# Storing a normalized operand by token class, and keys and values feature by feature

## The chip, the cores and the metric

The kernel runs on one core of a Trainium2 chip. The metric is the device time of one execution in microseconds; "us" below is always that. Three runs of the kernel before took 1931.80, 1932.94 and 1935.67 us, so the median is 1932.94 us. One further execution was recorded by the profiler, and every row below is from it.

The engines are named as in the profile: PE is TensorE (matmuls), PEld its loads of the stationary operand, DVE is VectorE, ACT is ScalarE, POOL is GpSimd, SP is SyncE, which issues most DMAs.

## The reference, cut to what matters

512 tokens of width 1024 pass through two stacks of layers. Only the first layer of the first stack is touched by the change. It normalizes the tokens and projects them:

```python
hn = rms_norm(h, norm_g[0])
q, k, v, gate_a, u, gate_b = split_cols(hn @ w_in, (512, 128, 128, 512, 512, 512))
q = rms_norm(q.reshape(b, L, 8, 64), q_g)
k = rms_norm(k.reshape(b, L, 2, 64), k_g)
att = swa_sink_attention(q, k, v, sinks, rel_bias) * silu(gate_a)
ssm = s5_mixer(u, log_dt, a_re, a_im, b_re, b_im, c_re, c_im, d, glu_w, glu_b) * silu(gate_b)
h = h + concatenate([att, ssm], axis=-1) @ w_out
```

`s5_mixer` is a linear recurrence over the tokens: 32 groups of 16 channels, 64 complex states each, `x[t] = A x[t-1] + B u[t]`, `y = Re(C x) + d u`, then a gelu and a gated product. The matrices A and B are worked out from small parameter tables (`log_dt`, `a_re`, `a_im`, ...) with exponentials, sines and powers. The rest of the network (a sparse attention layer, then two layers with forgetting and dilated attention and wide feed-forward parts) takes most of the time and isn't touched.

## The kernel before, in words

**Products.** Numbers are f32, split into a high and a low part in the engine's own 32-bit type. A product is three matmuls (`mm3`, lines 210, 211 and 212): high by high, high by low, low by high. There are two forms. In `tm` (token-major) 128 tokens of x are the stationary operand, and 256 weight columns move past it. In `fm` (feature-major) 128 weight columns are stationary, and the tokens move. With eight blocks of 128 input features, a `tm` of 128 tokens by 256 features is 24 matmuls. `slab` fetches 256 weight columns through two raw buffers on SP's queue and splits them: ACT makes the high part (line 204), DVE the low part (line 206).

**The operand.** `norm_block` scales a block of 128 tokens (`tb`, four of them), and `to_x` transposes it on PE into PSUM (line 266). ACT copies the high part to `xh` (line 268), and DVE subtracts to make `xl` (line 269). Column t of `x1` is token t.

**Order of the first layer.** The program text goes: for each block of tokens, normalize, project keys and values (`tm`, 24 matmuls), normalize the key heads (`head_norm`: ACT squares, DVE sums, POOL takes the power for 1/sqrt in 0.7 us, DVE scales, lines 394 to 399), transpose the keys to `kT` (line 436, tile `ft`); then the state space parameters: PE transposes the tables `prm` (line 460), DVE copies them to `pt` (line 462), and a long chain of small DVE and ACT operations makes the powers `pw`, the matrices `bb`, the tables `uu` and `et`, and at last `zb` (lines 466 to 614); meanwhile PE makes the state space input `u2` (192 matmuls). For this input the recurrence is cut in four token classes, token = 4 j + i, so the stationary operand of class i is every fourth column of `x1`:

```python
tm(ps[:, :256], w, lambda k: tuple(
    a[k // 4][:, k % 4].rearrange("p (j i) -> p i j", i=4)[:, i] for a in (x1.h, x1.l)))
```

Then follows the core of the state space layer in four quarters (`core_a`, `core_b`): `core_a(0)` transposes `zb` on PE (line 641) and makes the tile `c` (`c7`, line 650); the last half ends with the transposes of `gy` (line 735). After that come the queries (192 matmuls with a head norm for each block), the gates `gbt` and `gat` (192 matmuls with 512 moving columns, `fm`, then `silu2`, line 779), the gated product (its first matmul has `yh` as an operand), and the attention.

**What sets the order.** This text isn't executed as it stands. A scheduler fixes, when the program is built, one order for each engine, and fills gaps of one part with work of another: part of the query matmuls stand between those of the core. At run time each engine goes through its list strictly, and an instruction that waits holds all that stand behind it. Tiles come from pools with few buffers, and an accumulator (`acc`) in PSUM can be written again only when ACT or DVE has copied it out; for `u2` these copies are lines 358 (DVE) and 360 (ACT).

Of the kernel before, what the change touches and what calls it, by code (L numbers as in the profile page):

```python
# [8 lines left out]
F32 = mybir.dt.float32  # L9
# [88 lines left out]
def _build(tc, nc, ctx, t, out, dbg, upto):  # L98
# [158 lines left out]
        x.l = [xp.tile([128, 4, 512], F32R, tag="x", name="xl") for _ in range(2)]  # L257
        return x

    def to_x(xn, hdst, ldst, nk=8, tags=("tps", "tps")):  # L260

        for half in range(nk // 4):
            ps = pst(tags[half])
            pv = ps.rearrange("p (k t) -> p k t", k=4)
            for k in range(4):
                PE.transpose(pv[:, k], xn[:, (half * 4 + k) * 128:(half * 4 + k + 1) * 128], ident)
            h_ = hdst(half)
            A.activation(h_, pv, AF.Copy)  # L268
            V.tensor_tensor(ldst(half), pv, h_.bitcast(F32), op=OP.subtract)  # L269

    def norm_block(hb, gb, x, tb, tags=("tps", "tps"), pl=None, put_off=None):
        xn = (pl or nrm).tile([128, 1024], F32, tag="xn", name="xn")
        norm_scale(hb, gb, xn)
        sl = slice(tb * 128, (tb + 1) * 128)

        def rest():
            to_x(xn, lambda hf: x.h[hf][:, :, sl], lambda hf: x.l[hf][:, :, sl], tags=tags)
        if put_off:
            put_off(rest)
        else:  # L280
            rest()
# [78 lines left out]
            A.activation(dst, src, AF.Copy)  # L360


    st1 = ExitStack()
    l1 = phase(st1, "l1")
    n0x = ExitStack()
# [57 lines left out]
    V.tensor_copy(qgs, qg)  # L423
    V.tensor_scalar(qgs[:, 0:1], qg[:, 0:1], -0.125, None, op0=OP.mult)
    V.tensor_scalar(qgs[:, 2:3], qg[:, 2:3], -float(np.float32(128 ** -0.5)), None, op0=OP.mult)
    for tb in range(NB):
        norm_block(xin[tb], gb, x1, tb, pl=n0)
        sl = slice(tb * 128, (tb + 1) * 128)
        ps = acc()
        tm(ps[:, :256], w, xk(x1, tb * 128, tb * 128 + 128))  # L430
        kn2 = pj.tile([128, 2, 2, 64], F32, tag="kn2", name="kn2", bufs=2)
        head_norm(ps[:, :128], 2, 64, [kn2[:, :, q] for q in range(2)])
        evac(vt[:, tb], ps[:, 128:256])
        tp = pst("ft")
        for i in range(2):
            PE.transpose(tp[:, i * 128:(i + 1) * 128], kn2[:, i].rearrange("p a d -> p (a d)"), ident)
        A.activation(kT[:, :, sl], tp[:, :256].rearrange("p (a t) -> p a t", a=2), AF.Copy, scale=qgs[:, 1:2])
    bias_tables(n0, (sps(), sps()))
    n0x.close()
    dump("x1h", x1.h[0])  # L440
# [124 lines left out]
    w = 2  # L565
# [13 lines left out]
    for cs_ in range(2):  # L579
        w = slab(w_in1, 0, 8, [(1280 + cs_ * 256, 256)])  # L580
        for i in range(4):
            ps = acc()
            tm(ps[:, :256], w, lambda k: tuple(
                a[k // 4][:, k % 4].rearrange("p (j i) -> p i j", i=4)[:, i] for a in (x1.h, x1.l)))
            evac(u2[:, cs_ * 16:(cs_ + 1) * 16, i, :], ps[:, :256].rearrange("p (g x) -> p g x", x=16))
    dump("u2", u2)
    shm = nrm.tile([128, 1024], F32, tag="gb", name="shm").rearrange("p (t c) -> p t c", t=8)
# [170 lines left out]

    for cs_ in range(2):
        w = slab(w_in1, 0, 8, [(cs_ * 256, 256)])  # L760
        for tb in range(NB):
            sl = slice(tb * 128, (tb + 1) * 128)
            ps = acc()
            tm(ps[:, :256], w, xk(x1, tb * 128, tb * 128 + 128))
            qn = pj.tile([128, 4, 64], F32, tag="qn", name="qn", bufs=2)
            head_norm(ps[:, :256], 4, 64, [qn])
            steps.tick()
            steps.later(1, lambda a=(qn, cs_, sl): q_turn(*a))
# [6 lines left out]
    def silu2(pl, dst, ps):  # L775

        th_ = pl.tile([128, 512], F32, tag="th", name="th_", bufs=1)
        A.activation(th_, ps, AF.Tanh, scale=0.5)
        V.scalar_tensor_tensor(dst, th_, 1.0, ps, op0=OP.add, op1=OP.mult)

    gbt = ytp.tile([128, 4, 512], F32, name="gbt")
    for cs_ in range(2):
# [827 lines left out]
```

## Time and profile before

| What | Value |
| --- | --- |
| Median of three runs | 1932.94 us |
| Profiled execution, its own time | 1937.1 us |
| Span of its records | 1935.2 us |
| Mean granted TensorE clock | 0.971 |
| PE busy | 1833.9 us, 95% of the span, 11098 instructions |
| DVE busy | 1039.4 us, 54% |
| ACT busy | 728.6 us, 38% |
| POOL busy | 132.9 us, 7% |
| DMA | 161.74 MB, mean 84 GB/s |
| Chain that ended last | PE 81%, DVE 7%, issue 4%, DMA 3%, ACT 3%, POOL 1% |

Read it so: PE is busy nearly all the time, so the kernel as a whole hangs on PE, and the chain that ended last runs through PE for four fifths of the span. But these are averages over the whole network. The change touches about the first 220 us, and there the limits are different in each stretch; they have to be read from the rows of those stretches. The profiled execution is 4.2 us longer than the median (1937.1 against 1932.94 us).

### The profile page before, as it was taken

The numbers are of one execution on the slowest core, as the hardware profiler recorded it, in microseconds if no ns is written. First come the engines' busy times: TensorE is split into PE (matmuls) and PEld (weight loads), VectorE is DVE, ScalarE is ACT, GpSimd is POOL, SyncE is SP. The second block draws the span as 40 slices with busy tenths as digits, with TensorE's granted clock in tenths as the row PEclk, the third lists the DMA queues.
The fourth block names the chain that finished last, engine by engine and source line by source line (L and its number), as shares of the span: only waits on it lengthen the run. The fifth ranks groups of instructions, "written<-read, shape, count | busy, mean of one in ns | idle before, by whom it ended". The sixth has DMA issues, their size and how long they took to land.

```text
span 1935.2 us, 27920 instructions
## 1 busy us (share of the span) xinstructions
PE 1833.9 (95%) x11098; PEld 1540.4 (80%) x11100; DVE 1039.4 (54%) x2199; ACT 728.6 (38%) x1454; POOL 132.9 (7%) x151
## 2 busy tenths in 40 slices
PE   6999969999999999999999999999989899999998
PEld 5987759859789887678888888889957788888886
DVE  5874474268664534664655553366275555555522
ACT  4133353333443334543443341233264444333421
POOL 1332001203120000000000000000000000000000
PEclk9999989969999999989999999999999999999999
DMA  6112321301521432102333322333220043322321
GB/s 207 44 34 88 131 66 51 98 22 56 166 72 41 149 109 77 33 1 66 110 100 88 101 74 98 110 130 98 78 87 1 3 120 98 99 87 82 115 87 66
DMA packets 187898, 161.74 MB, mean 84 GB/s; under 512 B 14568, under 2 KB 170320, under 8 KB 187768
## 3 DMA queue, kind: packets, MB, share of 16 engines
q1 hardware_dynamic: 181168, 144.30, 24.1%
q0 software_dynamic: 2784, 9.00, 1.5%
q10 hardware_dynamic: 3816, 6.66, 1.0%
q8 instruction: 88, 1.44, 0.3%
q14 instruction: 42, 0.34, 0.1%
HBM read 157.88 MB, written 4.74 MB: 84 GB/s over the span
## 4 chain that ended last, share of the span: by engine, by line
PE 81%; DVE 7%; issue 4%; DMA 3%; ACT 3%; POOL 1%; ACTq 0%; POOLq 0%; DVEq 0%; SPq 0%
PE acc L212 19%; PE acc L210 19%; PE acc L211 19%; PE misc L338 6%; PE o L338 3%; PE tps L338 2%; PE spp L338 2%; DVE wl L206 1%; PE sps L1064 1%; PE misc L210 1%; PE misc L211 1%; PE misc L212 1%; PE o L1140 1%; ACT wh L204 1%; DVE xn L247 1%
## 5 line engine op out<-in xcount | busy, mean ns | idle before, releaser
L206 DVE TENSOR_TENSOR wl<-raw,wh 128x1024 fp32r<-128x1024 f32 (+3 forms) x250 | 299.1, 1207 | 408.2 <-ACT wh L204 407.3
L204 ACT ACTIVATE wh<-raw 128x1024 fp32r<-128x1024 f32 (+2 forms) x262 | 270.3, 1044 | 475.6 <-PE acc L211 208.9
L212 PE MATMUL acc<-xh,wl 128*128 128x512 f32 (+2 forms) x1032 | 391.0, 380 | 4.3 <-DVE wl L206 4.3
L210 PE MATMUL acc<-xh,wh 128*128 128x512 f32 (+2 forms) x1032 | 391.6, 381 | 0.7 <-ACT xh L268 0.5
L211 PE MATMUL acc<-xl,wh 128*128 128x512 f32 (+2 forms) x1032 | 391.0, 380 | 0.0
L212 PEld LDWEIGHTS acc<-xh,wl 128*128 128x128 f32 (+1 forms) x1032 | 193.9, 188 | 45.0 <-DVE wl L206 5.9
L210 PE MATMUL acc<-wh,xh 128*128 128x256 f32 (+1 forms) x736 | 224.5, 305 | 3.0 <-ACT xh L268 2.8
L210 PEld LDWEIGHTS acc<-xh,wh 128*128 128x128 f32 (+1 forms) x1032 | 193.1, 188 | 40.7 <-ACT xh L268 1.0
L211 PEld LDWEIGHTS acc<-xl,wh 128*128 128x128 f32 (+1 forms) x1032 | 193.8, 188 | 38.0
L211 PE MATMUL acc<-wl,xh 128*128 128x256 f32 (+1 forms) x736 | 220.6, 300 | 1.1 <-DVE wl L206 1.1
L212 PE MATMUL acc<-wh,xl 128*128 128x256 f32 (+1 forms) x736 | 220.2, 300 | 0.8 <-DVE xl L269 0.8
L210 PEld LDWEIGHTS acc<-wh,xh 128*128 128x128 f32 x736 | 152.5, 207 | 10.1 <-ACT xh L268 5.8
L212 PEld LDWEIGHTS acc<-wh,xl 128*128 128x128 f32 x736 | 152.7, 208 | 6.0 <-issue 4.3
L211 PEld LDWEIGHTS acc<-wl,xh 128*128 128x128 f32 x736 | 152.7, 207 | 4.9 <-issue 3.3
L212 PE MATMUL acc<-wh,gl 128*128 128x512 f32 x352 | 139.2, 395 | 0.0
L210 PE MATMUL acc<-wh,gh 128*128 128x512 f32 x352 | 138.6, 394 | 0.0
L211 PE MATMUL acc<-wl,gh 128*128 128x512 f32 x352 | 138.6, 394 | 0.0
L245 POOL TENSOR_TENSOR rs<-ss,mhalf 128x1 f32<-128x1 f32 x32 | 17.6, 552 | 1479.2 <-DVE ss L243 1470.2
L338 PE MATMUL misc<-wh,ah 128*128 128x256 f32 x280 | 83.0, 296 | 0.0
L338 PE MATMUL misc<-wl,ah 128*128 128x256 f32 x280 | 80.1, 286 | 0.0
L338 PE MATMUL misc<-wh,al 128*128 128x256 f32 x280 | 79.9, 285 | 0.0
L211 PEld LDWEIGHTS acc<-wl,gh 128*128 128x128 f32 x352 | 66.2, 188 | 15.6
(1494 smaller groups left out, 3057.1 us busy)
## 6 DMA issues: line engine op xcount, KB each, us to landing
raw<-in_w_up_dram SPq DMA_DIRECT2D x176, 256.0 KB, 3.1
raw<-in_w_down_dram SPq DMA_DIRECT2D x44, 512.0 KB, 3.6
raw<-in_od_w_in_dram SPq DMA_DIRECT2D x24, 512.0 KB, 3.5
raw<-in_w_in_dil_dram SPq DMA_DIRECT2D x20, 512.0 KB, 3.6
raw<-in_ev_w_in_dram SPq DMA_DIRECT2D x18, 512.0 KB, 4.0
raw<-in_w_out_dram SPq DMA_DIRECT2D x16, 512.0 KB, 3.9
raw<-in_w_in_fox_dram SPq DMA_DIRECT2D x14, 512.0 KB, 4.8
raw<-in_ev_w_out_dram SPq DMA_DIRECT2D x8, 512.0 KB, 4.2
```

The costliest lines, as they stand in the source:

```text
L204: A.activation(hi[:, k0:k1], raw, AF.Copy)
L206: eng.tensor_tensor(lo[:, k0:k1], raw, hi[:, k0:k1].bitcast(F32), op=OP.subtract)
L210: pe.matmul(ps, lh, rh, start=first, stop=False)
L211: pe.matmul(ps, lh, rl, start=False, stop=False)
L212: pe.matmul(ps, ll, rh, start=False, stop=last)
L245: G.tensor_tensor(r, ss[:, 3:4], mhalf[:, :1], op=OP.pow)
L247: V.scalar_tensor_tensor(xn[:, hv[i]], hb[:, hv[i]], r, gb[:, hv[i]], op0=OP.mult, op1=OP.mult)
L338: self.last = op(*a, **k).ins
L1064: PE.matmul(ps[:, :n], qiT[rw, hd // 2, qs], kiT[rw, :n], start=True, stop=True)
L1140: PE.matmul(pov[:, hd % 4], vt[:, kb, kv * 128:(kv + 1) * 128], pt_[:, kb * 128:(kb + 1) * 128], start=kb == 0, stop=kb == qb)
```

## The change

1. The first layer's operand `x1` is stored by token class: column i * 128 + tb * 32 + j holds token 4 (32 tb + j) + i. So the copies to `xh` and `xl` read PSUM with every fourth element and write 32 neighbouring columns for each class (`norm_block1`, and the new argument `view` of `to_x`).
2. The state space input takes `xk(x1, i * 128, i * 128 + 128)`, neighbouring columns, as its stationary operand. Its 192 matmuls remain 192.
3. Keys and values are now made for two blocks of tokens at a time, in feature-major form: 24 matmuls for the keys and 24 for the values with 256 moving tokens, 96 in all as before. The result is copied from PSUM into token order (`kvf`, 4 copies), and 8 transposes on PE (line 462 of the changed kernel) bring it back to tokens by features; head norm and the rest follow as before.
4. The queries run over classes instead of blocks, and their transposed result goes to every fourth column of `qT`.
5. `silu2` writes its result back into token order (8 operations on 128x512 elements, with a stride of four elements).

Behind the change, lines have other numbers: 460 is now 492 (tables), 490 is 522 (first power), 614 is 645 (`zb`), 641 is 672, 650 is 681, 735 is 766, 755 is 786.

```diff
-    def to_x(xn, hdst, ldst, nk=8, tags=("tps", "tps")):
+    def to_x(xn, hdst, ldst, nk=8, tags=("tps", "tps"), view=lambda a: a):
...
+            pv = view(pv)
             h_ = hdst(half)
             A.activation(h_, pv, AF.Copy)
             V.tensor_tensor(ldst(half), pv, h_.bitcast(F32), op=OP.subtract)
...
+    def by_i(ap):
+
+        return ap.rearrange("p (j i) -> p i j", i=4)
+
+    def norm_block1(hb, gb, x, tb, pl):
+        xn = pl.tile([128, 1024], F32, tag="xn", name="xn")
+        norm_scale(hb, gb, xn)
+
+        def dst(a):
+            return a.rearrange("p k (i t j) -> p t k i j", i=4, t=NB)[:, tb]
+        to_x(xn, lambda hf: dst(x.h[hf]), lambda hf: dst(x.l[hf]),
+             view=lambda pv: pv.rearrange("p k (j i) -> p k i j", i=4))
+
+    def xhalf(x, half):
+
+        return lambda k: tuple(a[k // 4][:, k % 4].rearrange("p (i j) -> p i j", i=4)[:, :, half * 64:half * 64 + 64]
+                               for a in (x.h, x.l))
...
-    for tb in range(NB):
-        norm_block(xin[tb], gb, x1, tb, pl=n0)
-        sl = slice(tb * 128, (tb + 1) * 128)
-        ps = acc()
-        tm(ps[:, :256], w, xk(x1, tb * 128, tb * 128 + 128))
...
+    for half in range(2):
+        for tb in (2 * half, 2 * half + 1):
+            norm_block1(xin[tb], gb, x1, tb, n0)
+        kvf = []
+        for part in range(2):
+            ps = acc()
+            fm(ps[:, :256].rearrange("p (i j) -> p i j", i=4), w, part * 128, 128, xhalf(x1, half))
+            f_ = n0.tile([128, 256], F32, tag=f"kvf{part}", name="kvf", bufs=1)
+            evac(by_i(f_), ps[:, :256].rearrange("p (i j) -> p i j", i=4))
+            kvf.append(f_)
+        for q in range(2):
+            tb = 2 * half + q
+            sl = slice(tb * 128, (tb + 1) * 128)
+            ps = sps()
+            for part in range(2):
+                PE.transpose(ps[:, part * 128:(part + 1) * 128], kvf[part][:, q * 128:(q + 1) * 128], ident)
...
-            tm(ps[:, :256], w, lambda k: tuple(
-                a[k // 4][:, k % 4].rearrange("p (j i) -> p i j", i=4)[:, i] for a in (x1.h, x1.l)))
+            tm(ps[:, :256], w, xk(x1, i * 128, i * 128 + 128))
...
-        for tb in range(NB):
-            sl = slice(tb * 128, (tb + 1) * 128)
+        for i in range(4):
+            sl = slice(i, 512, 4)
             ps = acc()
-            tm(ps[:, :256], w, xk(x1, tb * 128, tb * 128 + 128))
+            tm(ps[:, :256], w, xk(x1, i * 128, i * 128 + 128))
...
-        V.scalar_tensor_tensor(dst, th_, 1.0, ps, op0=OP.add, op1=OP.mult)
+        th_, ps = (a.rearrange("p (i j) -> p i j", i=4) for a in (th_, ps))
+        V.scalar_tensor_tensor(by_i(dst), th_, 1.0, ps, op0=OP.add, op1=OP.mult)
```

The scheduler's order changes with it in three places that matter below. In the rows, a name's number is that of its buffer, the operands stand as moving, then stationary, and "x3" is three instructions in a row.

First, PE's list where the tables `prm` are transposed, which opens the chain of small operations. Before, it stands among the key and value matmuls of the second block of tokens (`acc_254`):

```order
L172 MATMUL sps_426<-oh_427,rel_429 8x128
L210 MATMUL acc_254<-wh_133,xh_105 128x256
L211 MATMUL acc_254<-wl_134,xh_105 128x256
L460 MATMUL sps_447<-ident_90,prm_125 128x16 x3
L436 MATMUL ft_226<-ident_90,kn2_214 128x128 x2
L212 MATMUL acc_254<-wh_133,xl_107 128x256
```

In the changed kernel the same transposes (line 492) stand behind the last keys (`ft_441`), inside the second accumulator of the state space input (`acc_670`):

```order
L468 MATMUL ft_422<-ident_90,kn2_410 128x128 x2
L172 MATMUL sps_445<-oh_447,rel_449 8x512
L468 MATMUL ft_441<-ident_90,kn2_429 128x128 x2
L172 MATMUL sps_446<-oh_447,rel_449 8x128
L210 MATMUL acc_670<-wh_634,xh_105 128x256
L211 MATMUL acc_670<-wl_635,xh_105 128x256
L492 MATMUL sps_467<-ident_90,prm_125 128x16 x3
L212 MATMUL acc_670<-wh_634,xl_107 128x256
```

So the tables have moved from the second of four blocks to the place behind all four.

Second, PE's list at the end of the state space input. Before, the transposes of `zb` follow its last matmul (`acc_816`) at once, and the first query (`acc_1470`) begins between them:

```order
L211 MATMUL acc_816<-wl_729,xh_106 128x256
L212 MATMUL acc_816<-wh_728,xl_108 128x256
L641 MATMUL tps_871<-ident_90,zb_846 128x128 x4
L647 MATMUL sps_883<-cbd_524,zb_846 128x32
L210 MATMUL acc_1470<-wh_1460,xh_105 128x256
```

In the changed kernel 71 query matmuls (`acc_1490`, `acc_1525` and 23 of `acc_1564`) stand ahead of the same transposes, now line 672:

```order
L211 MATMUL acc_1564<-wl_1481,xh_106 128x256
L672 MATMUL tps_891<-ident_90,zb_866 128x128 x4
L678 MATMUL sps_903<-cbd_544,zb_866 128x32
L212 MATMUL acc_1564<-wh_1480,xl_108 128x256
L786 MATMUL ft_1599<-ident_90,qn_1550 128x128 x2
```

What moved is query work, from behind the core to a place ahead of it. At the core's end (line 735, now 766) 54 query matmuls and all 192 gate matmuls stood behind it before; now no query matmul does, and 174 gate matmuls.

Third, DVE's list in the changed kernel, in the middle of the chain of small operations (`uu`, `et`). The copy of `acc_810`, a finished accumulator of the state space input, stands there; its buffer is the one that the first query, `acc_1490`, is to use:

```order
L537 TENSOR_TENSOR et_555<-ctmp_587,ctmp_588 128x16x4
L590 SCALAR_TENSOR_TENSOR uu_494<-uu_494 128x16
L359 COPY u2_633<-acc_810 128x16x16
L591 TENSOR_TENSOR uu_494<-sc_473 128x16
L534 TENSOR_TENSOR ctmp_597<-et_555,uu_494 128x256
```

The copy comes behind the sixth squaring of `uu` (line 590), far down the chain. Two head norms of queries stand in the same list further on, ahead of the first `zb`; before, none did.

SP's list is the same but for one place: the load of `dm` (the table with d, 256 KB) stands behind two more weight loads (`raw_1482` and `raw_1486`, 512 KB each) than before.

## Rows read from the trace of the kernel before

**Rows 1.** Chain of waits (start, duration, engine, tile, line), 87 to 97 us.

```profile
87.31 0.23 PE acc L212
...
92.44 0.44 PE tps L641 x4
```

**Rows 2.** Busy time of each engine (instructions), granted clock, DMA share, GB/s, three stretches.

```profile
40.00:42.00 2.00, 2.00 (x11) 2.00 (x11) 0.00 (x0) 0.22 (x1) 0.00 (x0) 0.50 1.06 372
...
60.00:70.00 10.00, 10.00 (x44) 10.00 (x45) 9.83 (x16) 0.38 (x1) 9.61 (x9) 1.00 0.00 0
...
100.00:160.00 60.00, 56.66 (x669) 48.22 (x670) 45.95 (x95) 20.71 (x35) 20.23 (x21) 0.97 0.15 45
```

**Rows 3.** Groups by line, 60 to 92 us: the state space input's matmuls and weight loads.

```profile
L210 PE MATMUL acc<-wh,xh 128*128 128x256 f32 x46 | 18.2, 396 | 0.0
...
L210 PEld LDWEIGHTS acc<-wh,xh 128*128 128x128 f32 x46 | 15.2, 330 | 0.0
```

**Rows 4.** Timeline of TensorE and its loads: keys and values, then the state space input.

```profile
40.15 0.41 PE L210 MATMUL acc<-wh,xh 128*128 128x256 f32 x1
...
41.86 0.41 PE L212 MATMUL acc<-wh,xl 128*128 128x256 f32 x1
...
42.27 0.28 PE L211 MATMUL acc<-wl,xh 128*128 128x256 f32 x1
...
43.10 0.28 PE L212 MATMUL acc<-wh,xl 128*128 128x256 f32 x1
...
42.51 0.19 PEld L211 LDWEIGHTS acc<-wl,xh 128*128 128x128 f32 x1
...
56.33 0.40 PE L212 MATMUL acc<-wh,xl 128*128 128x256 f32 x1
...
59.84 0.40 PE L212 MATMUL acc<-wh,xl 128*128 128x256 f32 x1
```

**Rows 5.** Timeline of VectorE, 43 to 96 us, with idle time and releaser.

```profile
43.88 0.69 DVE L572 TENSOR_TENSOR dm<-dm,mkd 128x512 f32<-128x512 f32 x1 [5.72 <-DMA dm<-in_ev_ssm_d_dram]
...
44.49 0.18 DVE L490 TENSOR_TENSOR pw<-sc 128x16 f32<-128x16 f32 x1
...
83.97 0.69 DVE L614 TENSOR_TENSOR zb<-ctmp 128x512 f32<-128x512 f32 x1
...
86.02 0.69 DVE L614 TENSOR_TENSOR zb<-ctmp 128x512 f32<-128x512 f32 x1
...
92.48 0.42 DVE L358 COPY u<-acc 128x256 f32<-128x256 f32 x1 [5.77 <-PE acc L212]
...
95.41 0.29 DVE L650 TENSOR_TENSOR c<-sps,dm 128x128 f32<-128x128 f32 x1 [1.31 <-PE sps L647]
```

**Rows 6.** Timeline, 23 to 39 us: TensorE, then ScalarE.

```profile
23.41 0.35 PE L460 MATMUL sps<-ident,prm 16*128 16x16 f32 x3
...
37.62 0.69 PE L436 MATMUL ft<-ident,kn 128*128 128x128 f32 x2 [4.24 <-DVE kn L399]
...
33.95 0.22 ACT L466 ACTIVATE sc<-pt 128x16 f32<-128x16 f32 x1
...
38.72 0.20 ACT L482 ACTIVATE sc<-sc 128x16 f32<-128x16 f32 x1
```

**Rows 7.** Single lines' instructions, strided and contiguous writes: shortest, median and longest ns.

```profile
L740 DVE TENSOR_TENSOR yl<-tps,yh x4: 1075/1103/1169, 135.2 to 164.7; 128x512 fp32r<-128x512 f32 x4
...
L269 DVE TENSOR_TENSOR xl<-tps,xh x24: 677/680/692, 14.2 to 1573.2; 128x512 fp32r<-128x512 f32 x24
```

**Rows 8.** Timeline of TensorE, 161 to 218 us.

```profile
161.78 1.09 PE L735 MATMUL tps<-ident,gy 128*128 128x128 f32 x8 [0.91 <-DVE gy L728]
...
174.56 0.41 PE L755 MATMUL ft<-ident,qn 128*128 128x128 f32 x2 [1.32 <-DVE qn L399]
...
217.04 0.40 PE L212 MATMUL acc<-xh,wl 128*128 128x512 f32 x1
217.27 0.40 PE L210 MATMUL acc<-yh,wh 128*128 128x512 f32 x1
```

More of the change, by code (lines that the diff above doesn't have):

```diff
@@ L425, in _build @@
     V.tensor_scalar(qgs[:, 2:3], qg[:, 2:3], -float(np.float32(128 ** -0.5)), None, op0=OP.mult)
-    for tb in range(NB):
-        norm_block(xin[tb], gb, x1, tb, pl=n0)
-        sl = slice(tb * 128, (tb + 1) * 128)
-        ps = acc()
-        tm(ps[:, :256], w, xk(x1, tb * 128, tb * 128 + 128))
[L431 to L437, printed above, removed]
+    for half in range(2):
[14 more added lines that the diff above has]
+                PE.transpose(ps[:, part * 128:(part + 1) * 128], kvf[part][:, q * 128:(q + 1) * 128], ident)
+            kn2 = pj.tile([128, 2, 2, 64], F32, tag="kn2", name="kn2", bufs=2)
+            head_norm(ps[:, :128], 2, 64, [kn2[:, :, r] for r in range(2)])
+            evac(vt[:, tb], ps[:, 128:256])
+            tp = pst("ft")
+            for i in range(2):
+                PE.transpose(tp[:, i * 128:(i + 1) * 128], kn2[:, i].rearrange("p a d -> p (a d)"), ident)
+            A.activation(kT[:, :, sl], tp[:, :256].rearrange("p (a t) -> p a t", a=2), AF.Copy, scale=qgs[:, 1:2])
     bias_tables(n0, (sps(), sps()))
```

## The prediction

> **What bounds the kernel now.** I read the chain of waits first: ahead of 92 us it runs through the matmuls of the state space input, link after link of `acc`, and on into the transposes of `zb`, the core's first step [rows 1]. So in this stretch PE is the path. The view by windows agrees: from 60 to 70 us PE and its weight loads are busy for 10.00 of 10.00 us at a granted clock of 1.00 [rows 2], which is TensorE's upper level, 2.4 GHz. DVE is nearly as full there (9.83 us), with the chain of small operations that makes `zb`; that is the second candidate for the bound. Its timeline says how close it is: it starts with line 490 at 44.49 us (queued behind `dm`, whose DMA it waited 5.72 us for), ends the first `zb` at 83.97 + 0.69 = 84.66, the second at 86.02 + 0.69 = 86.7, and then DVE is idle for 5.77 us until PE gives it the last accumulator at 92.48 [rows 5]. PE reaches the core 7.6 us after `zb` is there. A faster PE is worth that much in this place, and anything beyond it only if DVE's chain is earlier too.
>
> Next the matmuls themselves. For the state space input, one of 128x256 takes 396 ns and its weight load 330 ns [rows 3], and they follow each other every 0.234 us: 15 steps from 56.33 to 59.84. The same shape for keys and values, whose stationary columns are neighbours, follows every 0.119 us, 7 steps from 42.27 to 43.10, with a load of 0.19 us [rows 4]. The Trainium skill's page "TensorE: Matmul & The Clock Gate", section "LDWEIGHTS (loading the stationary operand)", lets a load's time hang on the number of its columns alone; by it both loads would take the same, and the change would save nothing here. The trace, with 330 and 190 ns for 128 columns each, doesn't agree.
>
> **What the change removes.** 192 x (0.234 - 0.119) = 22.1 us of PE time. That is for a clock of 1.00 only: at a granted clock of 0.50 (1.2 GHz, 40 to 42 us [rows 2]) neighbouring columns follow every 0.21 us (8 steps from 40.15 to 41.86 [rows 4]), so almost nothing is saved there.
>
> **What it adds on PE.** Eight 128x128 transposes: a pair takes 0.41 us [rows 8] to 0.69 [rows 6], so 1.6 to 2.8 us. The 96 key and value matmuls stay, with other operands.
>
> **What it adds on ACT and DVE.** The 8 + 8 copies to `xh` and `xl` read and write with gaps. Contiguous, `xl` takes 0.68 us; the nearest strided row is `yl`, 1.10 us for the same size [rows 7]. So each costs between nothing and 0.42 us more, and I price ACT's like DVE's (an estimate). I take half: only the writes of `yl` skip, with a wider gap. The page "Advanced Engine Details and Errata" of the Trainium skill, section "Memory Cachelines", says that PSUM is read in lines of two f32 values, so every fourth value is a new line; by it the upper price holds, some 7 us more in all, of which the path would carry about 4. No row before shows such a read. Four copies `kvf` (0.42 us each by the accumulator's copy [rows 5], up to 0.7 strided) lie on the key path. The strided `silu2`, 8 times at most 0.42 us more, lies on DVE under gate matmuls of 24 x 0.23 us per tile, and costs nothing; without that cover it would cost 3.4 us.
>
> **What it moves.** The tables `prm` are transposed at 23.41 us and used by ACT at 33.95 [rows 6]. In the new order they stand on PE behind all keys. My hand schedule, from rows of like instructions (estimates): keys and values now need two normalized blocks, so they begin at about 18.6 us; 48 matmuls at 0.21 falling to 0.12 end at 26.4; copies, transposes and head norm (POOL's power 0.7 among them) end near 30; DVE makes the last `xl` of the second half at 33.6; its 48 matmuls, first at 0.21, end at 41.1; then the copy, two weight splits of 1.2 us on DVE, head norm and transposes, with the state space input waiting behind the keys' transposes on PE. So the tables come at 48.3, the copy `pt` at 48.7, and the small chain from line 466 to line 482 (4.97 us from 33.95 to 38.92 [rows 6], with other work between, 4.1 without) leads to line 522 at 52.8. `dm` lands about then as well: it stood ready at 43.88, and is moved past two loads on SP (some 4 us each). Before, line 490 was at 44.49; **the chain starts 8.3 us later**. From there to the first `zb` it is 84.66 - 44.49 = 40.2 us as before; one key head norm moves out (-1.5, with its wait), one copy (0.4) and two query head norms (2.0) move in. First `zb`: 52.8 + 40.2 + 0.9 = 93.9; before it was 84.66.
>
> PE meanwhile: 192 x 0.119 = 22.9 us from 41.1, with some 3.7 for waits at the keys and the lower clock: done at 67.7. Then the first query needs the buffer of `acc_810`, whose copy stands behind the sixth squaring on DVE, 27.1 us into the chain: 52.8 + 27.1 = 79.9. So PE is idle for 12 us; the queries run from there to about 93, at 0.21 or 0.12 us each. **PE's bound goes over to DVE's chain.** The core's transposes come at 93.9 instead of 92.28. The tile `c` (95.41 before) needs the second `zb` too, at 96.0, and two short groups of matmuls behind it: 97.7.
>
> **The core and the tail.** From `c` to the last transposes of `gy` it took 161.78 + 1.09 - 95.41 = 67.5 us, with PE busy for 56.66 of 60 us [rows 2], so I let it hang on PE's work: 16 or 17 query matmuls fewer (-2.0), 18 gate matmuls more (18 x 0.23 = 4.1): 97.7 + 67.5 + 2.2 = 167.4, instead of 162.87. Behind that point stood 54 queries, with stalls for head norms (1.32 at 174.56) and the gates, whose run at 0.23 (217.04, 217.27) ends at 217.27 [rows 8]: 54.4 us. Now there are 174 gate matmuls: 174 x 0.23 = 40.0. The gated product begins at 207.4.
>
> **The sum.** 217.27 - 207.4 = **9.9 us** gained; of 22.1 saved on PE, 12 go to the later chain. Later layers keep their order but for pieces; I give them nothing, and 2 us of uncertainty. The profiled execution's 1937.1 becomes 1927.2; it stands 4.2 above the median, which goes from 1932.94 to 1923.0. About 0.2%, 3.9 us, can be told from no change: faster is below 1929.1, slower above 1936.8.
>
> The bounds: with the tables transposed as soon as PE is through at the upper clock, line 522 comes at 48, and 14.7 us are gained; with all strided copies and the lower clock on the path it comes at 58, and 4.7 are gained. The own range of this case is 1918 to 1928.
>
> **The rivals.**
> - *PE stays the path.* If the scheduler's late places cost little at run time and the chain starts within 4 us of before, the core starts at 85 to 89 us and nearly all of the 22 us arrive: 1911 to 1918. For it: DVE was idle for 5.77 us. Against it: the order itself, tables behind all keys. Chance 0.12.
> - *The loss eats the gain.* Line 522 at 58 to 66: gain 4.7 to -3.7, 1928 to 1936.6. For it: the keys' path has POOL powers, two groups of waits (4.24 us at 37.62 [rows 6] before), and PE idles into its lower clock. Chance 0.17.
> - *Slower*, by one mechanism: the copies that read PSUM with gaps. All of ACT's and DVE's copies stand in series ahead of both halves of keys. At 1.1 us they add 4; to pass 66.6 us, from which it is slower than 1936.8, they must add 13.8, that is 1.7 us for each of 8 pairs, about twice the strided row's whole excess for both engines. Only if such reads are that much slower: about 1943 at 2.5 us. Chance 0.10.
> - *Stride isn't what makes the load slow.* Then the input stays at 192 x 0.234 = 44.9 us and ends at 89.7; 71 queries, ahead of the core now, lead to 98.0; the core ends 4 us later than forecast, and the gain is 5.8, only by the shorter tail: 1927. It is what the section on LDWEIGHTS named above would make of it; rows 4 speak against it. Chance 0.05.
> - My forecast: 0.56.
>
> Counted together: faster 0.72 (forecast, PE's path, the stride rival, a little of the second), within 0.2% 0.17, slower 0.11. The range 1912 to 1933 leaves out a part of the first rival and the slower half of the second with the third, 0.18 in all.
>
> **What would show it.** Right: loads of about 190 ns and a pitch of 0.12 in the input; a stretch of some 10 us before the core in which PE waits for a copy on DVE; line 522 at 48 to 58; `zb` (line 645) as the releaser of line 672; gates without queries behind line 766. Wrong: line 522 before 47 (more gain) or behind 60 (less); `xl` copies (line 270) of over 1.2 us; a core that takes longer than 70 us from line 681 to line 766, as queries and gates now sit elsewhere in it; or a gate run that stalls because its weights are split too late.

## The result, and the profile after

Four runs of the changed kernel took 1909.78 to 1915.12 us, with a median of 1912.51; four of the kernel before, on the same chip, 1931.80 to 1935.67, with a median of 1932.71. The ratio is 0.9895 [0.988, 0.9911]: 20.2 us faster. The direction is that of the forecast, but the forecast gain of 9.9 us is just under half of it, and the median lies below the forecast's own range of 1918 to 1928. The profiled execution took 1911.97 us.

The state space input first. The view by groups, 50 to 65 us of the changed kernel, PE and then its weight loads (count, busy us, mean ns of one, idle before):

```profile
L210 PE MATMUL acc<-wh,xh 128*128 128x256 f32 x43 | 12.1, 282 | 0.0
...
L210 PEld LDWEIGHTS acc<-wh,xh 128*128 128x128 f32 x42 | 8.0, 190 | 0.0
```

The load is 190 ns where it was 330 [rows 3]. The pitch follows: 128 matmuls of the three lines in 15 us are one every 0.117 us.

The windows of the changed kernel (busy us and count of PE, PEld, DVE, ACT, POOL; then the granted clock) show what came in its place:

```profile
50.00:60.00 10.00, 10.00 (x86) 10.00 (x85) 9.44 (x50) 3.33 (x7) 3.25 (x4) 1.00 0.91 276
60.00:70.00 10.00, 6.45 (x54) 6.24 (x53) 9.69 (x16) 2.66 (x4) 9.61 (x8) 0.94 0.29 94
70.00:75.00 5.00, 0.00 (x0) 0.00 (x0) 4.93 (x12) 0.00 (x0) 4.76 (x6) 0.50 0.00 2
75.00:80.00 5.00, 3.33 (x15) 3.33 (x16) 4.90 (x19) 0.00 (x0) 0.98 (x1) 0.50 0.00 0
```

PE is full to 60 us and then does nothing from 70 to 75, at the lower clock; DVE is nearly full in each row. PE's timeline names the wait (in brackets the idle time before, and what ended it):

```profile
76.67 0.58 PE L210 MATMUL acc<-wh,xh 128*128 128x256 f32 x1 [10.22 <-DVE u L359]
```

PE waits 10.22 us for the copy of the accumulator that the order put behind the sixth squaring. DVE's timeline has this copy and the steps of the chain around it:

```profile
50.49 0.19 DVE L522 TENSOR_TENSOR pw<-sc 128x16 f32<-128x16 f32 x1 [0.59 <-ACT sc L513]
...
76.21 0.41 DVE L359 COPY u<-acc 128x256 f32<-128x256 f32 x1
...
90.26 0.68 DVE L645 TENSOR_TENSOR zb<-ctmp 128x512 f32<-128x512 f32 x1
...
95.24 0.29 DVE L681 TENSOR_TENSOR c<-sps,dm 128x128 f32<-128x128 f32 x1 [0.72 <-PE sps L678]
```

Against [rows 5], the chain starts 6.0 us later, `zb` is 6.3 later, and `c` 0.2 earlier: the state space input is no longer what the core waits for. What is gained shows behind the core, in PE's timeline:

```profile
161.76 1.03 PE L766 MATMUL tps<-ident,gy 128*128 128x128 f32 x8
...
202.54 0.40 PE L210 MATMUL acc<-yh,wh 128*128 128x512 f32 x1
...
240.42 1.51 PE L339 MATMUL tps<-ident,s 128*128 128x128 f32 x6 [12.14 <-DVE s L943]
```

The core ends as before [rows 8], the gated product begins at 202.54, not 217.27, and the attention's first transposes come at 240.42; before, the same came at 254.70. So the first layer is 14.3 us shorter at that point, and the span, 1910.2 us, is 25.0 shorter (more than the 20.2 of the medians, as the profiled execution of the kernel before is a long one). **The other 10.7 us fell behind 240 us, where the diff touches nothing.** That is the question for the experiments.

The operand's copies from PSUM with gaps (`xh`, `xl`), priced at half of a strided operation's excess, cost nothing more. The view of lines 270 and 811 in the changed kernel (ns min/median/max, first and last start):

```profile
L270 DVE TENSOR_TENSOR xl<-tps,xh x24: 677/682/693, 13.8 to 1548.2; 128x512 fp32r<-128x512 f32 x24
...
L811 DVE SCALAR_TENSOR_TENSOR gbt<-th__1849,acc x1: 1082/1082/1082, 165.8 to 165.8; 128x512 f32<-128x512 f32 x1
```

Eight of the 24 `xl` read every fourth value, and no one takes longer than 693 ns; `silu2`, which writes every fourth value, takes 1082 (0.68 to 0.69 before). The rule on PSUM's lines that the prediction named, from the Trainium skill's page "Advanced Engine Details and Errata", section "Memory Cachelines", speaks of matmuls that slow down; carried over to copies, as the prediction did, it would have made the first kind slower. In these copies (682 ns, with gaps or without) the trace doesn't show that.

### The profile page after: what moved, and what is told of

Read it like the earlier page. It is cut to its first block, busy times and chain, and to the rows that moved or that the text cites. A ratio compares the mean times of both kernels' runs of the same rounds, so it can differ in the third digit from the quotient of the medians.

```text
span 1910.2 us, 27945 instructions
## 1 busy us (share of the span) xinstructions
PE 1806.0 (95%) x11106; PEld 1512.9 (79%) x11108; DVE 1043.8 (55%) x2201; ACT 731.5 (38%) x1456; POOL 139.3 (7%) x151
## 4 chain that ended last, share of the span: by engine, by line
PE 76%; DVE 10%; issue 5%; ACT 4%; DMA 3%; POOL 2%; ACTq 0%; POOLq 0%; DVEq 0%; SPq 0%
PE acc L212 19%; PE acc L210 19%; PE acc L211 19%; PE misc L339 6%; PE o L339 3%; PE tps L339 2%; PE spp L339 2%; DVE wl L206 2%; PE sps L1096 1%; ACT wh L204 1%; PE misc L210 1%; POOL rstd L234 1%; PE misc L211 1%; PE misc L212 1%; ACT p L1409 1%
## 5 line engine op out<-in xcount | busy, mean ns | idle before, releaser
L212 PE MATMUL acc<-xh,wl 128*128 128x512 f32 (+2 forms) x1064 | 400.4, 377 | 4.9 <-DVE wl L206 4.9
L210 PE MATMUL acc<-xh,wh 128*128 128x512 f32 (+2 forms) x1064 | 401.1, 379 | 1.2 <-ACT wh L204 0.7
L211 PE MATMUL acc<-xl,wh 128*128 128x512 f32 (+2 forms) x1064 | 400.5, 377 | 1.2 <-DVE xl L270 1.0
L210 PEld LDWEIGHTS acc<-xh,wh 128*128 128x128 f32 (+1 forms) x1064 | 199.8, 189 | 41.0 <-ACT wh L204 1.1
L210 PE MATMUL acc<-wh,xh 128*128 128x256 f32 (+1 forms) x704 | 206.5, 294 | 12.3 <-DVE u L359 10.2
L212 PE MATMUL acc<-wh,xl 128*128 128x256 f32 (+1 forms) x704 | 202.9, 288 | 0.6 <-DVE xl L270 0.6
L211 PE MATMUL acc<-wl,xh 128*128 128x256 f32 (+1 forms) x704 | 201.7, 287 | 0.9 <-DVE wl L206 0.9
L210 PEld LDWEIGHTS acc<-wh,xh 128*128 128x128 f32 x704 | 136.2, 193 | 17.5 <-DVE u L359 10.4
L212 PEld LDWEIGHTS acc<-wh,xl 128*128 128x128 f32 x704 | 136.2, 193 | 5.7 <-issue 4.4
L211 PEld LDWEIGHTS acc<-wl,xh 128*128 128x128 f32 x704 | 136.3, 194 | 1.8 <-DVE wl L206 1.1
```

The source lines that it names most:

```text
L210: pe.matmul(ps, lh, rh, start=first, stop=False)
L211: pe.matmul(ps, lh, rl, start=False, stop=False)
L212: pe.matmul(ps, ll, rh, start=False, stop=last)
```

## The experiments

Times are medians; each ratio is to the kernel before on the same chip. The runs are from several chips, on which the kernel before has medians of 1932.71 to 1937.81 us, so kernels of different chips are better compared by their ratios; that of the changed kernel is 0.9895 [0.988, 0.9911]. "Attention" is the start of the first attention transposes (254.70 us before, 240.42 changed), "rest" what follows it in the profiled execution (1680.5 and 1669.8).

### Where do 10 us come from behind 240 us?

Copies from PSUM are dealt by one counter that runs through the whole program:

```python
evq[0] += 1
if evq[0] % 3 == 0:
    V.tensor_copy(dst, src)
else:
    A.activation(dst, src, AF.Copy)
```

The change makes four such copies more (`kvf`), so every later copy of the program gets the turn of the one after it: another third of them is on DVE. Three kernels turn the deal back or on, at the first layer's end:

```diff
+    evq[0] -= 4      # e1, in the changed kernel
+    evq[0] += 4      # e2, in the kernel before
+    evq[0] += 4      # e5, in the changed kernel: the third turn
     hp = pool(ctx, "hp", 1, side="right")
```

> The changed kernel, with the counter that hands PSUM copies to DVE (every third) or ACT set back by 4 ahead of the gated product. The change makes 4 more such copies (the kvf tiles), so everything behind the first layer has its copies on other engines than before; here it has them as before, and the order of all later layers is again that of the kernel before. Theory (the turned rotation is where the time behind the first layer comes from): the stretch from the first attention transpose to the end goes from 1670 back to about 1680 us, and the median from 1912.5 to 1918 to 1923. Rival (the difference behind the first layer is only that between two executions): 1912.5, within 2. The first 225 us stay as they are by both.

Measured: 1922.95 us (1922.54 to 1924.16), ratio 0.9939 [0.9918, 0.996]. Attention stays at 240.59, the rest is 1680.1, that of the kernel before. The surplus behind the first layer is gone: against the changed kernel that is 8.5 us by the ratios and 10.4 by the medians. The median is the forecast's 1923.0, but on its own chip e1 gains 12.1 us, not 9.9.

> The kernel before, with the same counter set forward by 4 at the same place; nothing else. Theory (rotation): the first layer as before (first attention transpose at 254.7), the stretch behind it 1670 instead of 1680, median 1922 to 1927. Rival (executions differ): 1932.7, within 2.

Measured: 1923.47 (1922.52 to 1924.87), ratio 0.994 [0.9922, 0.9958]; attention 254.64, rest 1667.0. On one chip that is 11.6 us. So this part of the gain can be had without the change.

> The changed kernel with the copy counter moved on by one more step (4) ahead of the gated product: the third of the three possible turns; nothing else. First layer as in the changed kernel (first attention transpose at 240.4). Theory (each turn deals the copies of all later layers anew, and the time behind is a matter of that deal): the stretch behind differs again, by more than 3 us from both 1670 and 1680, or lies at one of them; no direction can be told beforehand: 1907 to 1925. Rival (the kernel before has the one bad turn, the other two are alike): within 2 of 1912.5.

Measured: 1917.33 (1912.64 to 1923.96), ratio 0.9894 [0.9869, 0.9919], as of the changed kernel; rest 1670.5. The rival held: of the three turns only that of the kernel before is the slow one. The other profiles bear it out: the three with the slow turn (the kernel before, e1 and e4) have a rest of 1680.0 to 1680.5 us, the eleven others 1663.0 to 1674.9. That spread also says how far a rest from one execution can be trusted: some 10 us between kernels with the same turn and the same code there.

Laid beside each other, e1 and the changed kernel keep step to some 500 us. In the forgetting attention they part, as the softmax's exponentials show (ns min/median/max, first and last start). The changed kernel:

```profile
L1409 ACT ACTIVATE p<-p,nm x48: 385/554/727, 735.3 to 852.8; 128x512 f32<-128x512 f32 x12, 128x384 f32<-128x384 f32 x12, 128x128 f32<-128x128 f32 x12, 128x256 f32<-128x256 f32 x12
```

e1:

```profile
L1410 ACT ACTIVATE p<-p,nm x48: 387/556/725, 736.7 to 856.9; 128x512 f32<-128x512 f32 x12, 128x384 f32<-128x384 f32 x12, 128x128 f32<-128x128 f32 x12, 128x256 f32<-128x256 f32 x12
```

The same 48 operations, none slower than its twin, take 117.5 us from first start to last, or 120.2. In the other two profiles with the slow turn they take 123.3 (the kernel before) and 124.6 (e4), in no other more than 118.4. PE's waits from 740 to 880 us (us in total, times, longest) say where such time goes. The changed kernel:

```profile
PE tps L339 <- DVE p L1414: 2.5, 7, 0.7
...
PE o L339 <- DVE al L1446: 0.6, 1, 0.6
```

e1:

```profile
PE tps L339 <- DVE p L1415: 5.1, 5, 1.9
...
PE o L339 <- DVE al L1447: 1.6, 2, 1.3
```

PE waits longer for DVE's normalization `p`. But these waits don't single out the slow turn: e5, which isn't slow, waits 3.9 us for `p` and 1.8 for `al` in the same window. By 900 us e1 and the changed kernel are some 6 us apart, and behind the dilated attention 10.5; some 4 of these came between 1250 and 1340 us, ahead of that attention's softmax. One more kernel tried to take DVE out of it: the copies of the last two attentions' transposes all on ACT (built on e10, below, with the counter running on):

```diff
-                evac(pt_[:, :m], tp[:, :m])
+                evq[0] += 1
+                A.activation(pt_[:, :m], tp[:, :m], AF.Copy)
```

> The kernel of the last call with the first two quarters' preparation on DVE, and in the second stack's two attention layers every copy of transposed weights (tile pt, line 1425 of the changed kernel) on ACT instead of two in three; the counter goes on, so all other copies stay where they are; nothing is left out. Theory (the deal matters because DVE is the later engine in these layers, and a copy that waits in its list holds PE up): DVE loses some 9 us of copies in the 118 us of the forgetting attention, PE's waits for DVE shrink, the stretch behind the first layer comes to 1662 to 1667 instead of 1670, the median 3 to 8 us below that kernel's. Rival (the copies only have to be spread evenly): ACT gets late with its exponentials, and the stretch is as long or longer, 1670 to 1680.

Measured: 1911.99 (1908.15 to 1914.78), ratio 0.9875 [0.9856, 0.9894]; e10 has 0.9844 [0.9819, 0.9869], so it isn't faster than e10, and by the ratios 6 us slower, with intervals that overlap. The rest is 1674.9 (e10: 1671.9), within the rival's 1670 to 1680. PE's waits from 757 to 880 us, e12:

```profile
PE tps L339 <- DVE p L1415: 5.3, 3, 2.2
PE o L339 <- DVE al L1448: 2.1, 2, 1.5
```

With none of these copies on DVE, PE waits for DVE's `p` as long as in e1 (e10: 2.6 us). DVE's busy time from 740 to 900 us fell from 97.6 (e10) to 86.7, and the rest didn't shrink. Besides, each turn gives DVE a third of the copies. So more load on DVE doesn't explain the slow turn; the rival, that the spread over both engines is what counts, fits better, but isn't shown. Which copy of which turn is the harmful one stays open.

### Which part of the change gains in the first layer?

e4 is the kernel before with neighbouring columns as the stationary operand, and nothing else:

```diff
-            tm(ps[:, :256], w, lambda k: tuple(
-                a[k // 4][:, k % 4].rearrange("p (j i) -> p i j", i=4)[:, i] for a in (x1.h, x1.l)))
+            tm(ps[:, :256], w, xk(x1, i * 128, i * 128 + 128))
```

> The kernel before, but the state space input takes 128 neighbouring columns (wrong tokens, as the operand is stored in order); all orders are unchanged. Theory: the input is done near 71 us, PE then waits for DVE's chain; the core starts when zb is there (84.7) instead of 92.3, 7.6 us earlier; what follows is as before, since the queries still stand behind: median about 1925. Rival (PE is the path): all 22 us, 1911. Rival (stride is free): 1932.7.

Measured: 1930.73 (1928.29 to 1935.12), ratio 0.9978 [0.9966, 0.999], 4.4 us. Attention 249.37, a gain of 5.3. Less than expected, for PE got ahead of everything: its waits from 40 to 100 us,

```profile
PE acc L210 <- DVE u L358: 9.9, 2, 8.0
PE ft L436 <- DVE kn L399: 6.2, 1, 6.2
```

are 16.1 us for DVE, and from 75 to 80 us its clock was 0.50. The core started at 87.02, against 92.28.

e9 is the kernel before with the new form of keys and values, and with the engine orders of the changed kernel; the operand stays in token order, and the input strided:

```diff
-    for tb in range(NB):
-        norm_block(xin[tb], gb, x1, tb, pl=n0)
...
+    for half in range(2):
+        for tb in (2 * half, 2 * half + 1):
+            norm_block(xin[tb], gb, x1, tb, pl=n0)
...
+            fm(ps[:, :256], w, part * 128, 128, xk(x1, half * 256, half * 256 + 256))
+            f_ = n0.tile([128, 256], F32, tag=f"kvf{part}", name="kvf", bufs=1)
+            evac(f_, ps[:, :256])
```

> Only one part of the change: keys and values feature by feature, two blocks at a time. The operand stays in token order, the state space input takes every fourth column, the gates are written plainly; all engines' orders are those of the changed kernel. Theory (the order that comes with the keys' form, queries ahead of the core, is worth some us; the new deal of copies is worth 10; the stride is worth the rest): against the kernel before on the same chip 0.992 to 0.994, and 5 to 7 us slower than the changed kernel. Rival (the keys' form costs what it delays, and the stride is all of the gain in the first layer): first layer longer than 254.7, median ratio 0.996 or more.

Measured: 1920.21 (1919.22 to 1923.47), ratio 0.992 [0.9896, 0.9944]. The turned deal is in it (rest 1666.8); attention is at 250.61, a gain of 4.1 in the first layer. The theory's 0.992 to 0.994 held.

e3 is the reverse of e4's edit, in the changed kernel:

```diff
-            tm(ps[:, :256], w, xk(x1, i * 128, i * 128 + 128))
+            tm(ps[:, :256], w, lambda k: tuple(
+                a[k // 4][:, k % 4].rearrange("p (j i) -> p i j", i=4)[:, i] for a in (x1.h, x1.l)))
```

> The changed kernel, but the state space input again takes every fourth column of the operand (wrong tokens, as the operand is now stored by class); all orders are unchanged. Theory (the stride alone makes the load slow, but DVE's chain bounds this stretch, so most of it is hidden): weight loads 330 ns, pitch 0.234, the input 22 us longer, its seventh accumulator ready only near 82, so that DVE waits some 5 us for it in the middle of the chain; the core some 5 to 6 us later, median about 1918. Rival A (PE is the path, all 22 come back): 1934. Rival B (stride is free): 1912.5.

Measured: 1919.13 (1916.08 to 1928.49), ratio 0.9927 [0.9902, 0.9951], some 6 us behind the changed kernel by the ratios, with intervals that overlap. The median is near the theory's 1918, but the profiled execution, the longest of the five at 1928.49, shows less hidden than the theory said: the core starts at 102.86, 11.9 us later and not 5 to 6, and attention is at 253.47, 13.1 later. Some 2 us of this are its own: its granted clock was 0.66 from 30 to 40 us, e9's 1.00. Groups of PE's loads, 65 to 90 us, e3:

```profile
L210 PEld LDWEIGHTS acc<-wh,xh 128*128 128x128 f32 x37 | 11.8, 319 | 0.0
```

With every order as in the changed kernel the load is 319 ns again, at the same granted clock of 1.00: the stride makes it, by a run that changes nothing else in the order or the shapes. e3 and e9 also show a second use of neighbouring columns that the forecast didn't count. DVE's timeline around the tables, in e9:

```profile
49.34 0.21 DVE L494 COPY pt<-sps 128x48 f32<-128x48 f32 x1 [4.63 <-PE sps L492]
...
54.96 0.19 DVE L522 TENSOR_TENSOR pw<-sc 128x16 f32<-128x16 f32 x1 [1.14 <-ACT sc L513]
```

and in the changed kernel:

```profile
46.37 0.21 DVE L494 COPY pt<-sps 128x48 f32<-128x48 f32 x1 [1.62 <-PE sps L492]
```

The tables are transposed inside the second accumulator of the state space input, so PE comes to them 3 us sooner when that input runs at 0.117, and line 522 is at 50.49, not 54.96. The two parts help each other: 5.3 us alone (e4), 4.1 alone (e9), 14.3 together, by the profiles. The windows from 0 to the start of the gated product say how (PE's busy time is the second figure of a row); the kernel before, e4, e9 and the changed kernel:

```profile
0.00:217.27 217.27, 189.20 (x1363) 167.62 (x1364) 135.48 (x320) 68.95 (x125) 55.99 (x59) 0.96 0.30 93
0.00:212.08 212.08, 171.25 (x1363) 149.30 (x1364) 135.60 (x320) 69.06 (x125) 56.05 (x59) 0.94 0.31 95
0.00:213.34 213.34, 189.22 (x1372) 166.65 (x1373) 137.50 (x322) 69.52 (x127) 61.63 (x59) 0.98 0.31 94
0.00:202.54 202.54, 167.99 (x1371) 145.22 (x1372) 140.19 (x322) 72.27 (x127) 62.96 (x59) 0.97 0.32 99
```

Neighbouring columns alone (e4) take 18.0 us off PE's busy time, and 12.8 of them come back as idle time (28.1 before, 40.8). The new order alone (e9) leaves the busy time and takes 4.0 off the idle time. Together the busy time falls by 21.2, and the idle time is only 34.5: the queries ahead of the core fill a part of the wait.

### Is DVE's chain the bound, and what sets it?

e6 takes away the wait of 10.22 us by copies of `u2` on ACT alone, e7 the late tables, and e8 both.

```diff
-            evac(u2[:, cs_ * 16:(cs_ + 1) * 16, i, :], ps[:, :256].rearrange("p (g x) -> p g x", x=16))
+            evq[0] += 1
+            A.activation(u2[:, cs_ * 16:(cs_ + 1) * 16, i, :], ps[:, :256].rearrange("p (g x) -> p g x", x=16), AF.Copy)
```

> The changed kernel, with all 8 copies of the state space input on ACT instead of 5 there and 3 on DVE; the counter goes on as before, so the deal behind stays. It takes the copy out of DVE's chain for which PE waits 10.2 us. Theory (DVE's chain decides when the core starts, PE's wait is slack): that wait is gone, the queries run from 66 us on, the core starts 1 to 2 us earlier, by three copies of 0.4 on DVE: median 1910.5 to 1911.5. Rival (PE's wait is the loss): 8 to 10 us less, 1903.

Measured: 1913.24 (1909.61 to 1920.31), ratio 0.9875 [0.9851, 0.9899], no difference from the changed kernel that can be told. PE's waits from 40 to 100 us:

```profile
PE ft L787 <- DVE qn L420: 17.0, 1, 17.0
```

The wait went from a copy to the head norm of a query, further on in DVE's list, and grew. Neither the small gain of the theory nor the 8 to 10 us of the rival came; in the profile the core starts 2.1 us later (93.10) and attention 4.3 later (244.69).

In e7 the tables stand ahead of the keys' loop in the text, down to the sines:

```diff
+    for i in range(3):
+        PE.transpose(prmps[:, i * 16:(i + 1) * 16], prm[:, i], ident[:16, :16])
+    pt = pp.tile([128, 3, 16], F32, name="pt")
...
+    A.activation(sn, rr, AF.Sin)
...
     for half in range(2):
         for tb in (2 * half, 2 * half + 1):
             norm_block1(xin[tb], gb, x1, tb, n0)
```

> The changed kernel, with the transposes of the parameter tables, the copy pt and the exponentials and sines written ahead of the keys and values; nothing is left out. PE's list now has the three transposes first, and 48 query matmuls ahead of the core instead of 71. Theory (the chain's late start costs what the stride gave): the first power (line 522) comes at 41 to 45 instead of 50.5, zb at 81 to 85 instead of 90.3, the core starts 6 to 9 earlier; 23 queries fall behind it (+2.7): median 1905 to 1909. Rival (something else sets the core's start): 1912.5.

Measured: 1919.13 (1914.33 to 1922.54), ratio 0.9899 [0.988, 0.9919]: no gain. The theory fell; DVE's timeline shows why:

```profile
50.10 0.49 DVE L420 TENSOR_TENSOR kn<-sps,rstd 128x128 f32<-128x128 f32 x2 [0.81 <-POOL rstd L234]
...
50.63 0.18 DVE L522 TENSOR_TENSOR pw<-sc 128x16 f32<-128x16 f32 x1
```

Line 522 now stands right behind the last keys' head norm, and that comes at 50.10, not 44.27, with the tables' work ahead of it. So the keys, too, hold the chain's start at 50 us. Attention comes at 246.92, 6.5 us later than in the changed kernel.

> Both together: tables first, and all copies of the state space input on ACT; nothing is left out. Theory: the core starts when zb is there, at 80 to 84, and PE has its 48 queries done by then: median 1903 to 1908, the fastest so far. Rival as for tables first: 1911 to 1912.5.

Measured, with both edits: 1919.96 (1916.56 to 1925.95), ratio 0.9916 [0.9895, 0.9937]; first `zb` at 91.86, attention at 245.94, 5.5 us later. No gain; the time is above the 1911 to 1912.5 of the rival, too. PE's timeline in e8 shows the bound itself:

```profile
92.61 1.12 PE L673 MATMUL tps<-ident,zb 128*128 128x128 f32 x4 [14.45 <-DVE zb L646]
```

With nothing else left to wait for, PE stands for 14.45 us until `zb`, the end of DVE's chain, is there.

What remains is the chain's own speed. Its small operations differ by a factor of six in the trace; the changed kernel's DVE from 65 us on,

```profile
65.34 1.20 DVE L596 COPY et<-uu 128x32 f32<-128x32 f32 x1
66.44 0.16 DVE L588 TENSOR_TENSOR sc<-uu 128x16 f32<-128x16 f32 x1
66.53 0.16 DVE L589 TENSOR_TENSOR sc<-uu 128x16 f32<-128x16 f32 x1
66.72 0.93 DVE L590 SCALAR_TENSOR_TENSOR uu<-uu 128x16 f32<-128x16 f32 x1
67.68 0.98 DVE L591 TENSOR_TENSOR uu<-sc 128x16 f32<-128x16 f32 x1
```

and POOL at the same time:

```profile
65.15 1.34 POOL L662 TENSOR_TENSOR cp<-gt 128x512 f32<-128x512 f32 x1
66.56 1.05 POOL L657 TENSOR_TENSOR gt<-pw,cc 128x512 f32<-128x512 f32 x1
67.58 1.06 POOL L658 TENSOR_TENSOR gt<-pw,cc 128x512 f32<-128x512 f32 x1
```

Between 66.49 and 66.56 POOL is free, and DVE does two operations at 0.16 us; the others end as POOL's do. e10 gives POOL's products of the first two quarters to DVE (its order has 95 queries ahead of the core instead of 71):

```diff
+            E_ = V if qu < 2 else G
-            G.tensor_tensor(ta, pwb(0), ccb(i), op=OP.mult)
+            E_.tensor_tensor(ta, pwb(0), ccb(i), op=OP.mult)
...
```

> The changed kernel, with the 12 operations of 128x512 that prepare the first two quarters (tiles gt and cp) on DVE instead of POOL; nothing is left out. While they run on POOL, some 15 of the chain's small operations take about 1 us instead of 0.17. Theory (POOL's work holds DVE up): those go back to 0.17 to 0.2, 12 us less; 12 operations of 0.68 come onto DVE, 8.2 more; zb at 86 to 87 instead of 90.3, 95 queries ahead of the core instead of 71, median 3 to 5 us below the changed kernel's. Rival (the small operations are slow by themselves): they stay at 1 us and zb comes at 98, 8 us slower.

Measured: 1905.13 (1902.93 to 1909.87), ratio 0.9844 [0.9819, 0.9869], the fastest kernel of this study; its interval lies below that of the changed kernel's ratio. The difference is 7.4 us by the medians and 9.9 by the ratios, more than the 3 to 5 expected. Groups of DVE, 44 to 92 us, e10:

```profile
L658 DVE TENSOR_TENSOR gt<-pw,cc 128x512 f32<-128x512 f32 x4 | 2.8, 700 | 0.0
...
L590 DVE SCALAR_TENSOR_TENSOR uu<-uu 128x16 f32<-128x16 f32 x8 | 1.4, 179 | 0.0
```

and of the changed kernel:

```profile
L590 DVE SCALAR_TENSOR_TENSOR uu<-uu 128x16 f32<-128x16 f32 x8 | 4.8, 600 | 0.1
```

The squaring takes 179 ns instead of 600, so DVE does POOL's work as well and still ends its chain sooner: from line 522 (52.73) to the first `zb` (88.61) it is 35.9 us, not 39.8. The gated product begins at 198.04, 4.5 earlier. (The profiled execution of e10, 1909.87, is the longest of its runs.) These 4.5 us aren't an earlier core: `c` comes at 94.99 instead of 95.24, and the last transposes of `gy` end at 163.16 instead of 162.79. They lie behind it, where 34.9 us of gate work are left instead of 39.75: ahead of the core PE waits once for DVE, 6.9 us, not 10.2 and 2.5, and does 24 query matmuls more. The edit brought this order with it, and no run takes the two apart. The Trainium skill's page "SBUF — State Buffer", section "SBUF: two separate sides", says that DVE and GpSimd share one pair of ports, which one of them holds for a whole instruction while the other waits; DVE needs the pair for operations with two inputs in SBUF, against a GpSimd operation that reads SBUF, or in a two-port mode. The two timelines above and the 179 ns agree with it.

Last, e11 moves the loop of the queries ahead of the core in the text, so that all 192 of their matmuls stand there:

```diff
-    core_a(0)
-    for qu in range(4):
...
         for i in range(4):
             sl = slice(i, 512, 4)
...
+    core_a(0)
+    for qu in range(4):
```

> The changed kernel, with all 192 query matmuls written and ordered ahead of the core instead of 71 ahead and 121 among it; nothing is left out. Theory (the core is bound by PE's work): the core starts 10 us later, at about 101, and is 12 to 14 us shorter; within 3 us of the changed kernel. Rival (the core hangs on its own chain, and queries in it are free): it keeps its 67.5 us, and the kernel is 9 to 10 us slower.

Measured: 1911.27 (1910.02 to 1913.11), ratio 0.9872 [0.9848, 0.9896], the same as the changed kernel. The core starts 19.1 us later (110.14), yet the attention only 2.6 later (243.06). The time is the theory's, the way isn't: the core took 65.9 us from `c` to the last transposes of `gy`, not 67.6 (the theory wanted 12 to 14 less), but from there to the gated product it was 26.7 us instead of 39.75, since gate matmuls had stood in for the queries in the core. Where PE's filling work stands changes little as long as there is enough of it.

## Why the prediction was right or wrong

**The stride is what makes the load slow: right.** A load of 190 ns and a pitch of 0.117 us, and 319 ns again with the stride alone put back (e3).

**PE's bound goes over to DVE's chain: right.** PE waited 10.22 us for the copy of `acc_810`, at 76.67; the forecast was a wait of 12 us, ending at 79.9. That DVE sets the core's start then is shown by e6 (a removed wait came back on another tile) and most plainly by e8 (14.45 us of waiting for `zb`). e10 adds that a faster chain pays, but through PE's shorter wait and the shorter tail, not through an earlier core.

**The first layer's sum: the mechanism right, three terms too large.** Line 522 was put at 52.8 and came at 50.49; this carries to `c`, 95.24 for 97.7: 2.5 us. The copy `pt` came at 46.37 for 48.7, and from there it took the 4.1 us of the forecast; so the keys' path of my hand schedule was too long, for one part, it seems, by the price of the copies with gaps. From `c` to the end of the core it was 67.6 us, not 67.5 + 2.2: 2.1 us. Gate matmuls more and queries fewer didn't lengthen it; PE's 56.4 of 60 busy us (100 to 160) were no fuller than before [rows 2]. The gates took 39.75 us for 40.0. Together 4.9 us: the gated product came at 202.54 for 207.4, and 14.7 us were gained there instead of 9.9. In PE's own account, 21.2 us of busy time went and 6.5 came back as idle time; the forecast had 22.1 and 12.

**The step that failed: "Later layers keep their order but for pieces; I give them nothing, and 2 us of uncertainty."** Their order is the same, but not the engine of their copies. Turned back, the changed kernel takes 1922.95 (e1); with its turn 1912.51, and the kernel before gains as much by the turn alone (e2). That is 8.5 us by the ratios, 10.4 by the medians and 10.5 by the profiles, in a term that the forecast put at nothing. Why the turn of the kernel before is the slow one stays open. e1 hit the forecast by chance in part: its first layer gained 14 by the profile, while the kernel before's profiled execution stood 4.2 above its median, and its chip was a slower one.

**The rivals.** That PE stays the path fell, though the time came out within its 1911 to 1918, by the turned deal and so by luck: line 522 came 6.0 us later, beyond the 4 that it asked for, and PE idled. That the loss eats the gain fell with line 522 at 50.49. That PSUM reads with gaps cost much fell with 682 ns. That the stride isn't the cause fell with 190 ns. Two slips in the working, without weight here: from 52.8 to 66 it is 13.2 us, so the slow end of the second rival is a loss of 3.3, not 3.7; and the chances of the forecast, of PE's path and of the stride rival come to 0.73 already, not 0.72.

## What to carry to other kernels

A counter that deals copies to engines in turn ties every part of a program to every call ahead: four copies in the first layer moved some 10 us in layers that nobody touched. Before a gain is put down to an edit, hold the deal fixed, or try every turn of it by itself. When one engine's chain becomes the bound, see first what makes its small operations slow; moving the waits around it (e6, e7, e8, e11) gave nothing that can be told by the ratios and cost 2.6 to 6.5 us in the first layer of the profiles, and taking POOL's work off its side gave 7 to 10 us together with the order that came with it. And look for the time that an engine is idle: what was saved in PE's matmuls counted only as far as other work of PE filled the wait behind it.

## What the runs showed of the hardware

A stationary operand of 128x128 with every fourth column takes 319 to 330 ns to load at a granted clock of 1.00, one with neighbouring columns 190. At 0.50 both take 330 in the kernel before (strided 52 to 54 us, neighbouring 40 to 41 us): the strided load is as slow at either clock. On DVE, a gap of four values cost nothing in reading from PSUM (0.68 us for 128x512) and 0.4 us in writing to SBUF (1.05 to 1.08 instead of 0.68). Operations of DVE on 128x16 took 0.16 us with POOL free and 0.9 to 1.3 when they met a product of 128x512 on POOL. Moving work onto DVE, the engine that was the bound, made its chain 3.9 us shorter (e10).
